# Three of four sums of weight blocks added by the loads themselves, and delayed sums of gated values, in a transformer trunk of two layers

## The chip, the cores and the metric

The kernel runs on one core of one Trainium2 chip. The metric is the device time of one execution in microseconds. TensorE (PE), VectorE (DVE), ScalarE (ACT), GpSimd (POOL) and SyncE (SP) each work through a program of their own; in this kernel SP and POOL also issue the DMAs spoken of here, each on a queue of its own.

## The reference

Two layers are applied to x, 1024 rows of 1024 values in float32; then a last normalisation.

```python
for l in range(DEPTH):
    x = x + hybrid_mixer(rms_norm(x, mix_norm[l]), ...)
    x = x + memory_cross_attention(rms_norm(x, mem_x_norm[l]), mem, ...)
    x = x + conv_gated_ffn(rms_norm(x, ffn_norm[l]), ffn_w_up[l], ffn_conv_w[l], ffn_conv_b[l], ffn_w_down[l])
return rms_norm(x, final_norm)

def conv_gated_ffn(h, w_up, conv_w, conv_b, w_down):
    a = h @ w_up
    ap = jnp.pad(a, ((0, 0), (1, 1), (0, 0)))
    a = ap[:, :-2] * conv_w[0] + ap[:, 1:-1] * conv_w[1] + ap[:, 2:] * conv_w[2] + conv_b
    gate, val = a[..., :D_FF], a[..., D_FF:]
    return (jax.nn.silu(gate) * val) @ w_down
```

The mixer has six latent attention heads, six grouped query heads and a gated part; D_FF is 2816.

## The kernel before

Each float32 operand is split into a high and a low part, and each product of two operands is three matmuls (high by high, high by low, low by high). The working memory in SBUF is 46 slots of 128 x 1024 floats, handed out by the class `Slots` in the order in which they came free. A framework schedules the program: it orders each engine's instructions itself, from the order of the code and the times that it reckons with, so code that moves in one place can reorder an engine elsewhere.

**A layer.** One combined projection comes first, then the attention: 24 items (12 heads by two groups of 512 queries) swept by `attention` (L332). Beside each item it runs side work from a table `fill`, and, in the third of an item's four steps, what the table `extra` holds for that item (L360). In an item POOL scales the rows of the probabilities (L305), which PE then transposes (L140). POOL also does parts of the rotary step for the coming heads (L621 to L627) and of the output's scaling (L682). Then come the output projection, the memory attention, and the FFN, in which the change lies.

**The FFN's up phase.** The two products of the FFN are each computed with seven block products in place of eight. w_up comes as four blocks b0 to b3, each 22 columns of 128 wide; a column is a tile of 128 x 512 floats, 256 KB. The seven products m = 1 to 7 of column j need on the side of the weights:

| m | weights | m | weights |
|---|---|---|---|
| 1 | b0 | 5 | b2 + b3 |
| 2 | b1 | 7 | b0 + b2 |
| 4 | b3 | 6 | b0 + b2 + b3 |
| | | 3 | b0 + b1 + b2 + b3 |

On the side of the activations `NormS.make(m)` forms sums and differences and splits them. The list `order` puts the products (j, m): columns 0 and 1 side by side at first, then a column after the other in the order 1, (4 of the column before), 6, 5, 2, 7, 3. One step of the loop at L1299 does this: `fetch()` (L1082) loads a column of 256 KB into half a slot; `make_w()` (L1091) makes the operand of the product four places on, its high part on ACT (L1096) and its low part on DVE (L1097); `product(j, m)` issues 12 matmuls (L1143 to L1145); `post(j, m)` takes the product out of its bank (ACT L1159 for m = 1, L1165 for m = 2; DVE for the others, L1171 for m = 7); and the convolution, the gating and `keep` of finished columns are worked off a list `todo`. Five columns are fetched before the FFN begins (FETCH - AHEAD), and two at a time in the first four steps.

**The sums of blocks.** `Blocks` (L781) computes all four sums ahead, in DRAM, in parts of two to four columns (up to 1 MB; UP_PARTS, DOWN_PARTS). For each sum and part SP copies one block (L796) and POOL adds another by a DMA that accumulates onto the copy (L801); 6 is made by adding 5, and 3 by adding 6. For w_up each layer runs 24 copies and 24 adds during its attention, from `extra`. For w_down (11 columns, parts of 3, 4 and 4) it runs 12 copies in the attention, and the 12 adds come later, one at every product m = 5 of the up phase from column 2 on (`add_later`). The copies carry a dependence on the last L305 in the code so that the scheduler doesn't issue them sooner. POOL does little else in the FFN: the reciprocal roots of the norm (L132) and the issuing of DMAs.

**The gated values.** `keep(j)` (L1210) stores the gated column's halves to DRAM by SP (L1213), seven stores for each pair of columns, and forms four sums of those pieces by accumulating DMAs on POOL (L1216), issued right behind the stores in the code.

**The down phase.** `down` goes through (m, i), 11 columns i for each m in the order 1, 5, 6, 3, 7, 2, 4. `fetch_d` (L1223) loads a piece of the gated values and a column of w_down or of its sums, eight places ahead; `make_d` (L1230) splits both on ACT and DVE, four places ahead; `d_mm` (L1252) does the 12 matmuls (L1256).

Of the kernel before, what the change touches and what calls it, by code (L numbers as in the profile page):

```python
# [8 lines left out]
F32 = mybir.dt.float32  # L9
F32R = mybir.dt.float32r  # L10
AF = mybir.ActivationFunctionType
ALU = mybir.AluOpType
AX = mybir.AxisListType

P = 128
# [54 lines left out]
def trunk(ctx: ExitStack, tc: tile.TileContext, a: dict, out: bass.AP):  # L70
# [313 lines left out]
    def layer(l, nt, w_m, last):  # L384
# [396 lines left out]
        class Blocks:  # L781

            def __init__(self, w, parts, name):
                self.w, self.parts, self.at = w, parts, [sum(parts[:i]) for i in range(len(parts))]
                self.sum = {
                    (m, i): dpool.tile([P, n * CH + 16], F32, tag=f"{name}{l}_{m}_{i}", name=f"{name}{l}_{m}_{i}")[:, : n * CH]
                    for m in (5, 6, 7, 3) for i, n in enumerate(parts)
                }  # L790

            def piece(self, b, i):
                return self.w[b][:, self.at[i] * CH : (self.at[i] + self.parts[i]) * CH]

            def copy(self, m, i):
                c = nc.sync.dma_start(self.sum[m, i], self.piece({5: 2, 6: 0, 7: 0, 3: 1}[m], i))  # L796
                tc.add_manual_dep(ins_of(c), ins_of(Item.last).name, mybir.DependencyInfo(mybir.DependencyClass.Sync, mybir.DependencyReason.DATA), reason="not sooner")

            def add(self, m, i):
                src = self.sum[{6: 5, 3: 6}[m], i] if m in (6, 3) else self.piece({5: 3, 7: 2}[m], i)  # L800
                tc.keep_in_program_order(nc.gpsimd.dma_start(self.sum[m, i], src, accum_op=ALU.add))  # L801

            def block(self, m, j):
                if m in (1, 2, 4):
                    return self.w[{1: 0, 2: 1, 4: 3}[m]][:, j * CH : (j + 1) * CH]
                i = max(i for i in range(len(self.parts)) if self.at[i] <= j)
                return self.sum[m, i][:, (j - self.at[i]) * CH : (j - self.at[i] + 1) * CH]

            def steps(self):
                n = len(self.parts)  # L810
                return [(self, m, i + o) for i in range(0, n, 2) for m, o in ((5, 0), (5, 1), (7, 0), (6, 0), (6, 1), (7, 1), (3, 0), (3, 1)) if i + o < n]

# [56 lines left out]

        extra, steps = {}, w_u.steps()  # L870
        for n, (w, m, i) in enumerate(steps):
            g = n * 18 // len(steps)
            extra.setdefault(g, []).append(lambda w=w, m=m, i=i: w.copy(m, i))
            extra.setdefault(g + 3, []).append(lambda w=w, m=m, i=i: w.add(m, i))
        later = deque(sorted(w_d.steps(), key=lambda s: (5, 7, 6, 3).index(s[1])))
        for n, (w, m, i) in enumerate(later):
            extra.setdefault(n * 20 // len(later), []).append(lambda w=w, m=m, i=i: w.copy(m, i))

        def add_later():
            if later:  # L880
                w, m, i = later.popleft()
                w.add(m, i)

# [198 lines left out]
        def fetch():  # L1082

            if (jm := next(fetched, None)) is not None:
                if not half:
                    z = sl.get(F32)
                    half.extend([(quarter(z, 0), None), (quarter(z, 1), z)])
                raws[jm] = half.pop(0)
                nc.sync.dma_start(raws[jm][0], w_u.block(jm[1], jm[0]))

# [9 lines left out]

        for _ in range(FETCH - AHEAD):
            fetch()
# [107 lines left out]
        def keep(j):  # L1210
            z, i = st.pop(j)["cg"], j // 2
            for q, h in ((("21", 1), ("u4", 1), ("22", 0), ("u2", 0)) if j % 2 else (("11", 1), ("u1", 0), ("u3", 0))):
                nc.sync.dma_start(gq[q, i], quarter(z, h))  # L1213
            sl.put(z)
            for q, p in ((("u3", "22"), ("u2", "u1"), ("u4", "u2")) if j % 2 else (("u1", "11"),)):
                nc.gpsimd.dma_start(gq[q, i], gq[p, i], accum_op=ALU.add)  # L1216

# [5 lines left out]
        def fetch_d():  # L1223
            if (mi := next(d_fetch, None)) is not None:
                m, i = mi
                z = d_raw[mi] = sl.get(F32)
                nc.sync.dma_start(quarter(z, 0), gq[{1: "11", 2: "21", 3: "22", 4: "u4", 5: "u1", 6: "u2", 7: "u3"}[m], i])
                nc.sync.dma_start(quarter(z, 1), w_d.block(m, i))

# [34 lines left out]
        def down(after0, after1, tail):  # L1264

            for m, i in d_order:
# [20 lines left out]
                for _ in range(2):  # L1287
                    if todo:
                        todo.popleft()()
                if i == NP - 1:  # L1290
                    for t in range(TPC):
                        d_add(m, t)
                        if m == 7:
                            after0(t)
                    if m == 2 and tail:
                        tail(None)

        early = deque()
        for i, (j, m) in enumerate(order):  # L1299
            for _ in range(1 + (i < AHEAD)):  # L1300
                fetch()
            for _ in range(1 + (i < AHEAD)):
                make_w()
            product(j, m)
            post(j, m)
            if (j, m) == (0, 2):
                ns.turn(1, range(0, 4))
                ns.turn(1, range(4, 8))
                ns.make(5)
            if m == 5 and j > 1:  # L1310
                add_later()
# [190 lines left out]
```

## Time and profile before

| | |
|---|---|
| time, median of three runs | 2774.91 us (2772.91 to 2776.51) |
| profiled execution, its time | 2770.64 us |
| its span | 2768.8 us |
| granted clock | 0.998 |
| busy: PE, DVE, ACT, POOL | 98%, 70%, 53%, 26% |
| DMA packets' time on SP's queue, on POOL's | 34.6%, 18.2% of the engines' span |
| HBM read, written | 371.75 MB, 206.05 MB |

The profile is one execution, taken by the hardware profiler; its own time is compared with its span, not with the median. The windows view gives the busy time of each engine in a stretch of the span; the waits name what ended an engine's idle time; the chain is the work that ended last, followed back; the timeline lists an engine's instructions. Attention of the first layer runs from about 130 to 480 us of the span, of the second from 1505 to 1855; the up phase of the first layer's FFN from about 745 to 1175, its down phase up to 1385. L12 is line 12 of the kernel.

### The profile page before, as it was taken

To read this page: it belongs to the slowest core of one execution; us is meant where nothing else is said; L and a number is where in the kernel's file an instruction comes from. 1 tells how busy PE (TensorE), PEld (TensorE's weight loads), DVE (VectorE), ACT (ScalarE), POOL (GpSimd) and SP (SyncE) were. 2 spreads that over 40 slices of the span, in tenths; PEclk is the share of its full clock that TensorE was granted. 3 is DMA by queue.
4 is the path that set the end of the run, shared out by engine and by line. 5 is a ranking of instruction groups with operands and counts; after the bars stand their busy time and mean duration, and the time that the engine had idled before them with its cause. 6 is when DMAs were issued, how large, how long until landed. Compare 5 with 4: busy or idle time off the path is not lost.

```text
span 2768.8 us, 37951 instructions
## 1 busy us (share of the span) xinstructions
PE 2724.2 (98%) x13648; PEld 2284.4 (83%) x13648; DVE 1941.6 (70%) x2905; ACT 1470.8 (53%) x2838; POOL 706.3 (26%) x744
## 2 busy tenths in 40 slices
PE   9999999999999999999999999999999999999998
PEld 7997888888878888888889877888888888888887
DVE  5489879556697777774445888894666877778754
ACT  4378978224554444553333888881345544446432
POOL 3245676320001110000123456662200011100000
PEclk9999999999999999999999999999999999999999
DMA  4027994221159875785210289831221698767752
GB/s 147 27 80 199 263 233 97 73 69 62 46 150 237 223 213 166 225 272 183 88 59 19 83 232 265 220 83 61 70 68 46 173 239 225 204 169 244 247 187 102
DMA packets 160748, 418.80 MB, mean 151 GB/s; under 512 B 17840, under 2 KB 18480, under 8 KB 146224
## 3 DMA queue, kind: packets, MB, share of 16 engines
q1 hardware_dynamic: 137376, 323.84, 34.6%
q0 software_dynamic: 23040, 92.28, 18.2%
q8 instruction: 107, 1.75, 0.2%
q14 instruction: 81, 0.66, 0.1%
q10 hardware_dynamic: 144, 0.26, 0.0%
HBM read 371.75 MB, written 206.05 MB: 209 GB/s over the span
## 4 chain that ended last, share of the span: by engine, by line
PE 85%; DVE 5%; ACT 3%; DMA 3%; POOL 2%; issue 1%; SPq 0%; POOLq 0%; DVEq 0%; ACTq 0%
PE bank L1256 8%; PE bank L116 7%; PE bank L118 7%; PE bank L117 7%; PE bank L140 7%; PE pair L1256 6%; PE bank L1144 5%; PE bank L1145 5%; PE bank L1143 5%; PE pair L1143 4%; PE pair L1144 4%; PE pair L1145 4%; PE bank L318 3%; PE bank L319 3%; PE pair L116 2%; PE pair L118 2%
## 5 line engine op out<-in xcount | busy, mean ns | idle before, releaser
L124 DVE TENSOR_TENSOR s<-bank,s 128x512 fp32r<-128x512 f32 (+3 forms) x552 | 331.5, 630 | 116.4 <-ACT s L123 112.7
L116 PE MATMUL bank<-s,s 128*128 128x512 f32 (+4 forms) x1124 | 404.2, 360 | 4.6 <-DVE s L124 3.4
L118 PE MATMUL bank<-s,s 128*128 128x512 f32 (+4 forms) x1124 | 399.5, 356 | 1.1 <-DVE s L111 0.9
L117 PE MATMUL bank<-s,s 128*128 128x512 f32 (+4 forms) x1124 | 398.4, 355 | 0.3 <-DVE s L111 0.3
L123 ACT ACTIVATE s<-bank 128x512 fp32r<-128x512 f32 (+3 forms) x552 | 286.0, 556 | 205.7 <-PE bank L140 142.5
L140 PE MATMUL bank<-ident,s 128*128 128x128 f32 (+1 forms) x2320 | 324.0, 274 | 17.5 <-POOL s L305 6.3
L140 PEld LDWEIGHTS bank<-ident,s 128*128 128x128 f32 (+1 forms) x2320 | 270.1, 140 | 77.7 <-DVE s L124 9.6
L1096 ACT ACTIVATE s<-s 128x512 fp32r<-128x512 f32 x308 | 187.5, 627 | 181.5 <-PE bank L1145 46.1
L1144 PE MATMUL bank<-s,s 128*128 128x512 f32 x704 | 274.5, 390 | 0.9 <-DVE s L209 0.9
L1145 PE MATMUL bank<-s,s 128*128 128x512 f32 x704 | 273.9, 389 | 0.0
L1143 PE MATMUL bank<-s,s 128*128 128x512 f32 x704 | 273.7, 389 | 0.0
L305 POOL TENSOR_SCALAR s<-s,stat 128x1024 f32<-128x1024 f32 x192 | 222.8, 1160 | 184.4 <-DVE stat L304 136.5
L295 DVE TENSOR_REDUCE stat<-pair 128x1 f32<-128x1024 f32 x192 | 233.5, 1216 | 39.6 <-PE pair L118 19.0
L132 POOL TENSOR_TENSOR stat<-stat,mhalf 128x1 f32<-128x1 f32 (+3 forms) x94 | 84.3, 897 | 634.3 <-DVE stat L131 634.1
L1256 PE MATMUL bank<-s,s 128*128 128x512 f32 (+1 forms) x1068 | 242.7, 387 | 1.6 <-DVE stat L131 1.6
L116 PEld LDWEIGHTS bank<-s,s 128*128 128x128 f32 x1124 | 211.7, 189 | 33.6 <-DVE s L124 3.7
L1241 DVE TENSOR_TENSOR s<-s,s 128x512 fp32r<-128x512 f32 x264 | 170.6, 685 | 93.1 <-ACT s L1240 93.1
L1256 PEld LDWEIGHTS bank<-s,s 128*128 128x128 f32 x1068 | 198.7, 188 | 42.3 <-DVE x L1347 1.8
L118 PEld LDWEIGHTS bank<-s,s 128*128 128x128 f32 x1124 | 211.7, 188 | 26.3 <-DVE s L111 1.3
L117 PEld LDWEIGHTS bank<-s,s 128*128 128x128 f32 x1124 | 212.1, 189 | 24.1 <-DVE s L111 0.6
L1240 ACT ACTIVATE s<-s 128x512 fp32r<-128x512 f32 x264 | 153.9, 623 | 140.9 <-DMA s<-g_u 47.3
L1097 DVE TENSOR_TENSOR s<-s,s 128x512 fp32r<-128x512 f32 x308 | 201.7, 686 | 36.2 <-ACT s L1096 33.9
(182 smaller groups left out, 5521.0 us busy)
## 6 DMA issues: line engine op xcount, KB each, us to landing
s<-u SPq DMA_DIRECT2D x176, 256.0 KB, 4.3
u<-in_w_up SPq DMA_DIRECT2D x40, 1024.0 KB, 13.3
s<-in_w_up SPq DMA_DIRECT2D x132, 256.0 KB, 4.4
g_u<-s SPq DMA_DIRECT2D x88, 256.0 KB, 3.0
s<-g_u SPq DMA_DIRECT2D x88, 256.0 KB, 3.3
s<-d SPq DMA_DIRECT2D x88, 256.0 KB, 3.6
u<-in_w_up POOLq DMA_DIRECT2D x20, 1024.0 KB, 18.4
u<-u POOLq DMA_DIRECT2D x20, 1024.0 KB, 13.3
```

The lines of the kernel that those rows point to most:

```text
L116: nc.tensor.matmul(o, l[0], r[0], start=first, stop=False)
L117: nc.tensor.matmul(o, l[0], r[1], start=False, stop=False)
L118: nc.tensor.matmul(o, l[1], r[0], start=False, stop=last)
L123: nc.scalar.activation(hi, src, AF.Copy)
L124: nc.vector.tensor_tensor(lo, src, f(hi), ALU.subtract)
L140: nc.tensor.transpose(b[:m, j * P : (j + 1) * P], s, ident)
L295: nc.vector.reduce_max(self.nm[:, 0:1], s, axis=AX.X, negate=True)
L305: Item.last = nc.gpsimd.tensor_scalar(p, p, r[:, 0:1], 0.0, ALU.mult, ALU.add)
L1143: nc.tensor.matmul(o, lh, rh, start=k == 0 and m in (1, 5, 6), stop=False, skip_group_check=True)
L1144: nc.tensor.matmul(o, lh, rl, start=False, stop=False, skip_group_check=True)
L1145: nc.tensor.matmul(o, ll, rh, start=False, stop=k == 3, skip_group_check=True)
L1256: nc.tensor.matmul(o, lh[p], rh[q], start=m in (1, 5, 2) and i == 0 and k == 0, stop=i == NP - 1 and k == 2, skip_group_check=True)
```

## The change

Only the sum for m = 6 is still made ahead in DRAM: per part one copy of b0, then b2 and b3 added. For w_up that is 6 copies and 12 adds a layer, spread over the attention's items by another rule; for w_down 3 copies in the attention and 6 adds, one at the product m = 5 of every even column from 2 on. The three other sums are made when a column is loaded (`load`): SP loads one block's column into the slot (b2, b0, or the ready sum), and POOL accumulates the second (b3, b2, or b1) onto it from DRAM by a DMA. In all 66 such accumulations of 256 KB in the up phase of a layer and 33 in its down phase. `keep` puts its sums into a list `due`; `add_due` issues them three, six and nine steps later, both in the up and the down phase. And four columns, not five, are fetched before the FFN begins.

```diff
-            def copy(self, m, i):
-                c = nc.sync.dma_start(self.sum[m, i], self.piece({5: 2, 6: 0, 7: 0, 3: 1}[m], i))
+            def copy(self, i):
+                c = nc.sync.dma_start(self.sum[i], self.piece(0, i))
...
-            def add(self, m, i):
-                src = self.sum[{6: 5, 3: 6}[m], i] if m in (6, 3) else self.piece({5: 3, 7: 2}[m], i)
-                tc.keep_in_program_order(nc.gpsimd.dma_start(self.sum[m, i], src, accum_op=ALU.add))
...
+            def add(self, i, b):
+                tc.keep_in_program_order(nc.gpsimd.dma_start(self.sum[i], self.piece(b, i), accum_op=ALU.add))
...
+            def load(self, z, m, j):
+
+                first, *second = {1: (0,), 2: (1,), 4: (3,), 6: (4,), 5: (2, 3), 7: (0, 2), 3: (4, 1)}[m]
+                nc.sync.dma_start(z, self.col(first, j))
+                if second:
+                    nc.gpsimd.dma_start(z, self.col(second[0], j), accum_op=ALU.add)
...
-        extra, steps = {}, w_u.steps()
-        for n, (w, m, i) in enumerate(steps):
-            g = n * 18 // len(steps)
-            extra.setdefault(g, []).append(lambda w=w, m=m, i=i: w.copy(m, i))
-            extra.setdefault(g + 3, []).append(lambda w=w, m=m, i=i: w.add(m, i))
-        later = deque(sorted(w_d.steps(), key=lambda s: (5, 7, 6, 3).index(s[1])))
-        for n, (w, m, i) in enumerate(later):
-            extra.setdefault(n * 20 // len(later), []).append(lambda w=w, m=m, i=i: w.copy(m, i))
+        extra, later = {}, deque((w_d, i, b) for b in (2, 3) for i in range(len(DOWN_PARTS)))
+        for i in range(len(UP_PARTS)):
+            extra.setdefault(2 * i, []).append(lambda i=i: w_u.copy(i))
+            for n in range(2):
+                extra.setdefault(2 * i + 4 + 3 * n, []).append(lambda i=i, n=n: w_u.add(i, 2 + n))
+        for i in range(len(DOWN_PARTS)):
+            extra.setdefault(13 + 2 * i, []).append(lambda i=i: w_d.copy(i))
...
-                nc.sync.dma_start(raws[jm][0], w_u.block(jm[1], jm[0]))
+                w_u.load(raws[jm][0], jm[1], jm[0])
...
-        for _ in range(FETCH - AHEAD):
+        for _ in range(AHEAD):
             fetch()
...
-            for q, p in ((("u3", "22"), ("u2", "u1"), ("u4", "u2")) if j % 2 else (("u1", "11"),)):
-                nc.gpsimd.dma_start(gq[q, i], gq[p, i], accum_op=ALU.add)
+            for n, (q, p) in enumerate((("u3", "22"), ("u2", "u1"), ("u4", "u2")) if j % 2 else (("u1", "11"),)):
+                due.append((step[0] + 3 + 3 * n, lambda q=q, p=p, i=i: nc.gpsimd.dma_start(gq[q, i], gq[p, i], accum_op=ALU.add)))
+
+        due, step = deque(), [0]
+
+        def add_due(all=False):
+
+            while due and (all or due[0][0] <= step[0]):
+                due.popleft()[1]()
...
-                nc.sync.dma_start(quarter(z, 1), w_d.block(m, i))
+                w_d.load(quarter(z, 1), m, i)
...
+                step[0] += 1
+                add_due(not todo)
...
+            step[0] = i
             for _ in range(1 + (i < AHEAD)):
                 fetch()
+            add_due()
...
-            if m == 5 and j > 1:
+            if m == 5 and j > 1 and j % 2 == 0:
                 add_later()
```

In the kernel after, L801 of `Blocks.add` is L798, the loads of a column are L809 (SP) and L811 (POOL's accumulation), L1096 is L1095, L1159 and L1165 are L1158 and L1164, L1216 is L1215.

Three places show how the change moves instructions. The first is POOL in the first layer's attention, at one of the piles of work ahead of a scaling that PE waits for; u is a part of w_up's sums, s a slot, L682 and L621 to L627 the steps named above. Before:

```order
L801 DMA u_3_2_1629<-u_6_2_1617 128x2048
L305 TENSOR_SCALAR s_340_3877<-s_340_3877,stat 128x1024
L682 TENSOR_TENSOR s_318_3676<-s_318_3676,s_344_3928 128x1024
L621 TENSOR_TENSOR s_348_3966<-s_141_1705,s_73_703 128x128
L622 TENSOR_TENSOR s_348_3966<-s_141_1705,s_73_703 128x128
L623 TENSOR_TENSOR s_348_3966<-s_141_1705,s_73_703 128x128
L625 TENSOR_TENSOR s_348_3966<-s_141_1705,s_73_703 128x128
L626 TENSOR_TENSOR s_141_1705<-s_348_3966 128x8x16
L305 TENSOR_SCALAR s_343_3922<-s_343_3922,stat 128x1024
L627 TENSOR_TENSOR s_141_1705<-s_348_3966 128x8x16
L305 TENSOR_SCALAR s_347_3960<-s_347_3960,stat 128x1024
```

The same place on POOL after the change:

```order
L798 DMA u_3_1612<-in_w_up 128x2048
L305 TENSOR_SCALAR s_340_3824<-s_340_3824,stat 128x1024
L682 TENSOR_TENSOR s_318_3626<-s_318_3626,s_344_3874 128x1024
L621 TENSOR_TENSOR s_348_3912<-s_141_1678,s_73_703 128x128
L622 TENSOR_TENSOR s_348_3912<-s_141_1678,s_73_703 128x128
L623 TENSOR_TENSOR s_348_3912<-s_141_1678,s_73_703 128x128
L625 TENSOR_TENSOR s_348_3912<-s_141_1678,s_73_703 128x128
L626 TENSOR_TENSOR s_141_1678<-s_348_3912 128x8x16
L627 TENSOR_TENSOR s_141_1678<-s_348_3912 128x8x16
L305 TENSOR_SCALAR s_343_3868<-s_343_3868,stat 128x1024
L305 TENSOR_SCALAR s_347_3906<-s_347_3906,stat 128x1024
```

The DMA at the head stays with another source; L627 has moved ahead of the scaling behind which it stood.

The second place is POOL at the start of the first layer's FFN; L110 makes rows of the norm, L132 is the reciprocal root of a row block's mean square, g_u and d are sums of gated values and of w_down. Before:

```order
L110 TENSOR_SCALAR s_660_7281<-s_659_7280 128x1024
L110 TENSOR_SCALAR s_663_7287<-s_662_7286 128x1024
L132 TENSOR_TENSOR stat<-stat,mhalf 128x1 x8
L1216 DMA g_u_0_7786<-g_11_0_7753 128x512
L801 DMA d_5_0_1633<-in_w_down 128x1536
L1216 DMA g_u_0_7808<-g_22_0_7775 128x512
```

The same place on POOL after the change:

```order
L110 TENSOR_SCALAR s_660_7215<-s_659_7214 128x1024
L110 TENSOR_SCALAR s_663_7221<-s_662_7220 128x1024
L811 DMA s_698_7762<-in_w_up 128x512 x2
L132 TENSOR_TENSOR stat<-stat,mhalf 128x1 x7
L811 DMA s_706_7812<-in_w_up 128x512 x2
L811 DMA s_714_7901<-in_w_up 128x512 x2
L132 TENSOR_TENSOR stat<-stat,mhalf 128x1
L811 DMA s_732_8031<-in_w_up 128x512
L811 DMA s_740_8086<-in_w_up 128x512 x2
L811 DMA s_752_8180<-in_w_up 128x512
L798 DMA d_0_1615<-in_w_down 128x1536
```

Six accumulations, for the products (0, 5), (1, 5), (0, 3), (1, 3), (0, 7) and (1, 7), now stand ahead of the eighth L132, four of them directly.

The third place is ACT at the same time: it makes operands (L1096, after it L1095) between the copies of product banks (L1159 and L1165, after it L1158 and L1164). Before:

```order
L1159 ACTIVATE s_702_7852<-bank 128x512
L1096 ACTIVATE s_719_7989<-s_703_7855 128x512
L1096 ACTIVATE s_721_8008<-s_703_7855 128x512
L1096 ACTIVATE s_726_8046<-s_707_7879 128x512
L1159 ACTIVATE s_706_7876<-bank 128x512
L1096 ACTIVATE s_735_8112<-s_715_7966 128x512
L1165 ACTIVATE s_710_7899<-bank 128x512
L185 ACTIVATE s_681_7601<-bank,cols_86 128x512
```

ACT at that place after the change:

```order
L1158 ACTIVATE s_701_7786<-bank 128x512
L1095 ACTIVATE s_719_7928<-s_706_7812 128x512
L1095 ACTIVATE s_720_7946<-s_706_7812 128x512
L1095 ACTIVATE s_726_7985<-s_714_7901 128x512
L1158 ACTIVATE s_705_7810<-bank 128x512
L1164 ACTIVATE s_709_7835<-bank 128x512
L185 ACTIVATE s_680_7533<-bank,cols_86 128x512
```

The operand of slot s_714, the one for (0, 7), is made at the same place as before, but its block is now the sum of two transfers; the L185 that scale the turned rows stand two copies behind it. The operand between the two copies has moved further back.

More of the change, by code (lines that the diff above doesn't have):

```diff
@@ L786, in __init__ @@
                 self.w, self.parts, self.at = w, parts, [sum(parts[:i]) for i in range(len(parts))]
[L787 to L790, printed above, removed]
+                self.sum = [dpool.tile([P, n * CH + 16], F32, tag=f"{name}{l}_{i}", name=f"{name}{l}_{i}")[:, : n * CH] for i, n in enumerate(parts)]
@@ L803, in block @@
-            def block(self, m, j):
-                if m in (1, 2, 4):
-                    return self.w[{1: 0, 2: 1, 4: 3}[m]][:, j * CH : (j + 1) * CH]
-                i = max(i for i in range(len(self.parts)) if self.at[i] <= j)
[L807 to L811, printed above, removed]
+            def add(self, i, b):
+                tc.keep_in_program_order(nc.gpsimd.dma_start(self.sum[i], self.piece(b, i), accum_op=ALU.add))
@@ new lines, in col @@
+            def col(self, b, j):
+                if b < 4:
+                    return self.w[b][:, j * CH : (j + 1) * CH]
+                i = max(i for i in range(len(self.parts)) if self.at[i] <= j)
+                return self.sum[i][:, (j - self.at[i]) * CH : (j - self.at[i] + 1) * CH]
+            def load(self, z, m, j):
[3 more added lines that the diff above has]
+                    nc.gpsimd.dma_start(z, self.col(second[0], j), accum_op=ALU.add)
@@ L867, in layer @@
         fill[23] += [lambda: y_split(1, 1, 2)]
-        extra, steps = {}, w_u.steps()
-        for n, (w, m, i) in enumerate(steps):
-            g = n * 18 // len(steps)
-            extra.setdefault(g, []).append(lambda w=w, m=m, i=i: w.copy(m, i))
-            extra.setdefault(g + 3, []).append(lambda w=w, m=m, i=i: w.add(m, i))
-        later = deque(sorted(w_d.steps(), key=lambda s: (5, 7, 6, 3).index(s[1])))
-        for n, (w, m, i) in enumerate(later):
-            extra.setdefault(n * 20 // len(later), []).append(lambda w=w, m=m, i=i: w.copy(m, i))
+        extra, later = {}, deque((w_d, i, b) for b in (2, 3) for i in range(len(DOWN_PARTS)))
[5 more added lines that the diff above has]
+            extra.setdefault(13 + 2 * i, []).append(lambda i=i: w_d.copy(i))
         def add_later():
             if later:
-                w, m, i = later.popleft()
-                w.add(m, i)
+                w, i, b = later.popleft()
+                w.add(i, b)
         w_o = {}
```

## The prediction

> **What bounds the kernel now.** I read the page's head first, then the windows view by stage, then the waits, then the chain and the timeline where PE stands still.
>
> ```profile
> span 2768.8 us, 37951 instructions
> PE 2724.2 (98%) x13648; PEld 2284.4 (83%) x13648; DVE 1941.6 (70%) x2905; ACT 1470.8 (53%) x2838; POOL 706.3 (26%) x744
> ```
>
> PE is busy for 2724.2 of 2768.8 us, so 44.6 us is all that any change in the transfers can win, and the change removes no matmul. The windows view shows where that idle time lies (columns: stretch, its length, busy us and instructions of PE, PEld, DVE, ACT, POOL, granted clock, DMA share, GB/s):
>
> ```profile
> 130.00:480.00 350.00, 341.21 (x1960) 287.50 (x1959) 298.54 (x484) 283.89 (x620) 217.62 (x210) 1.00 0.65 170
> 756.00:860.00 104.00, 100.60 (x445) 81.53 (x445) 88.63 (x125) 57.70 (x85) 10.01 (x12) 1.00 0.65 174
> 860.00:1010.00 150.00, 150.00 (x660) 123.36 (x659) 108.66 (x141) 67.99 (x94) 19.90 (x24) 1.00 0.88 223
> 1010.00:1170.00 160.00, 160.00 (x704) 131.38 (x704) 117.03 (x155) 76.02 (x110) 13.13 (x16) 1.00 0.66 195
> 1505.00:1855.00 350.00, 341.65 (x1953) 287.56 (x1952) 298.48 (x483) 283.97 (x619) 215.74 (x210) 1.00 0.65 170
> ```
>
> The attention of each layer (first and last row) leaves PE idle for 8.8 and 8.4 us; the first 104 us of the FFN's up phase for 3.4; the 310 us behind them for nothing, though the DMA share reaches 0.88 there. So the attention can gain a little, and the up phase, where the change puts its new transfers, can only lose.
>
> **The change part by part.**
>
> *Attention: half of POOL's accumulating DMAs go.* A layer issues 12 in place of 24 here. The windows view of L801 alone, POOL's waits, and the place of PE's largest wait, by the chain and the timeline:
>
> ```profile
> 130.00:480.00 350.00, 20.11 (x24) 1.00 0.65 170
> PE bank L140 <- POOL s L305: 6.3, 4, 2.5
> 347.76 2.37 POOL s L682
> ...
> 352.21 1.12 POOL s L305
> 353.30 0.45 POOL L627 TENSOR_TENSOR s<-s 128x128 f32<-128x128 f32 x1
> 353.38 0.76 PE L140 MATMUL bank<-ident,s 128*128 128x128 f32 x5 [2.50 <-POOL s L305]
> 1727.36 1.14 PE L140 MATMUL bank<-ident,s 128*128 128x128 f32 x5 [2.50 <-POOL s L305]
> ```
>
> 24 issues hold POOL for 20.11 us, 0.84 each, so 12 fewer free 10.1 us of its 217.6. But PE waited for POOL only 6.3 us in the whole program, and 5.0 of that are the two waits of 2.50 us, one in each layer. What runs on POOL ahead of them is L682 (2.37 us), the small steps L621 to L626 and the scaling L305; no DMA stands in that chain, so taking DMAs out doesn't shorten it. By the order of instructions the step L627 (0.45 us) now stands ahead of the scaling that PE waits for, where it stood behind: +0.45 us a layer, +0.9 in all. For the other waits I take −1 us of the remaining 1.3 us on POOL, a little less than all of it. Bounds of this term: −6.3 (all waits on POOL go) and +3 (one more step of 0.84 to 1.12 us in each pile). Taken: −0.1.
>
> *Start of the FFN: the accumulations stand ahead of the last rows' norm on POOL.* The order puts six issues of L811 ahead of the eighth L132 (the reciprocal root of the last 128 rows), and the two for products (0,7) and (1,7) ahead of nothing but ACT. The timeline of before:
>
> ```profile
> 744.05 0.84 SPq L1089 DMA_DIRECT2D s<-u  x2
> 744.94 1.30 SPq L1089 DMA_DIRECT2D s<-in_w_up  x2
> 748.82 0.93 POOL L132 TENSOR_TENSOR stat<-stat,mhalf 128x1 f32<-128x1 f32 x1 [7.12 <-DVE stat L131]
> 749.23 1.68 ACT L1096 ACTIVATE s<-s 128x512 fp32r<-128x512 f32 x3
> 754.04 0.60 ACT L1165 ACTIVATE s<-bank 128x512 f32<-128x512 f32 x1 [0.44 <-PE bank L1145]
> 754.54 3.00 ACT L185 ACTIVATE s<-bank,cols 128x512 f32<-128x512 f32 x5
> s<-in_w_up SPq DMA_DIRECT2D x132, 256.0 KB, 4.4
> g_u<-g POOLq DMA_DIRECT2D x44, 256.0 KB, 5.5
> ```
>
> POOL had been idle 7.12 us ahead of that L132, so the first accumulations find room; the last two wait for loads issued at about 744.5 us, which land 4.4 us later (748.9). L132 behind them is late by about one issue, 0.84 us or a little over. The sum for (0,7) is there 5.5 us after its issue, at 754.4. By the new order ACT makes that operand's high part, then copies two product banks, then starts the eight L185 that split the turned rows. Three instructions of about 0.5 us from 754.4 put L185 at 755.9 in place of 754.54: +1.4 us a layer, +2.8 in all, since PE has no other work there (3.4 us idle in the window from 756). Bounds 0 (the loads are issued earlier than I think) and +3 a layer (one product's time more).
>
> *Up phase: 66 small accumulations a layer come in, six of w_down's twelve large sums go.* The DMA view of 860 to 1010 us, and the loads' margins:
>
> ```profile
> q0 software_dynamic: 3510, 12.25, 45.2%
> q1 hardware_dynamic: 11548, 21.03, 42.2%
> d<-d POOLq DMA_DIRECT2D x4, 1024.0 KB, 10.8
> d<-in_w_down POOLq DMA_DIRECT2D x2, 1024.0 KB, 10.1
> d<-d POOLq DMA_DIRECT2D x2, 768.0 KB, 9.3
> 1132.89 0.42 SPq L1089 DMA_DIRECT2D s<-in_w_up  x1
> 1156.62 0.62 ACT L1096 ACTIVATE s<-s 128x512 fp32r<-128x512 f32 x1
> 1172.49 0.39 PE L1143 MATMUL pair<-s,s 128*128 128x512 f32 x1
> 1175.37 29.92 PE bank L1256 x132
> ```
>
> Queue 0 (POOL's) held the engines for 45.2% of 150 us = 67.8 us for 12.25 MB, 5.53 us a MB, so a block of 256 KB (0.262 MB) costs 1.45 us. Queue 1 (SP's) took 63.3 us for 21.03 MB: 0.79 us a block. An accumulation onto a block in SBUF isn't in the trace. Its bounds: 0.79 (it costs a plain load), and 67.8 / 24 = 2.8 us, if all of queue 0's time went by the piece (POOL's 24 instructions in that window are its issues). I take 1.45: most of those pieces are accumulations of just this size on just this queue. Eight sums for w_down, 6 × 1.049 + 2 × 0.786 = 7.86 MB or 43.5 us, 29.0% of the window, become four or so: −14.5 points. Three accumulations every seven products come in: a product is 12 matmuls, 29.92 / 11 = 2.72 us, so 150 us hold 150 / 19.04 × 3 = 23.6 of them, 34.3 us, +22.8 points. Share: 87.4 − 14.5 + 22.8 = 95.7%. It fits, and reaches 100% at a price of (100 − 72.9)% × 150 / 23.6 = 1.72 us. With 0.79 the share would be 85%.
>
> What covers the longer way of a block: the last load of the phase goes out at 1132.89, is made into an operand at 1156.62 and multiplied from 1172.49. Of the 23.7 us up to ACT, the shorter lookahead (four fetches ahead in place of five) takes 2.7; load, issue and accumulation take 4.4 + 0.8 + 5.5 = 10.7. So 10.3 us are left before ACT would wait at all, and 15.9 more before PE would. Cost at the share of 0.96: 0.
>
> *Down phase: 33 accumulations a layer onto w_down's blocks.* The windows view and ACT's waits:
>
> ```profile
> 1170.00:1385.00 215.00, 214.28 (x951) 176.79 (x949) 128.04 (x200) 92.73 (x158) 12.47 (x15) 1.00 0.56 182
> ACT s L1240 <- DMA s<-g_u: 47.3, 29, 3.5
> ```
>
> The share is lower (0.56), blocks are fetched as far ahead as before, and ACT already waits for loads here (47.3 us) while PE stands only 0.7 us of 215: the operands are made well ahead. Cost 0, or up to the 0.7 us again in each layer.
>
> *The late loads of 853 us.* PE's only other stops in the up phase:
>
> ```profile
> 853.49 0.50 PE L1143 MATMUL pair<-s,s 128*128 128x512 f32 x1 [1.52 <-DVE s L1171]
> 2228.45 0.50 PE L1143 MATMUL pair<-s,s 128*128 128x512 f32 x1 [0.48 <-DVE s L1171]
> s<-in_w_up SPq DMA_DIRECT2D x4, 256.0 KB, 9.6
> d<-in_w_down POOLq DMA_DIRECT2D x2, 1024.0 KB, 12.9
> ```
>
> The last two rows are the DMA view of 820 to 845 us: loads took 9.6 us beside two sums of 1 MB, and 8 us later PE waited. With half as many such sums I take half of 1.52 + 0.48 back: −1.0 (bounds −2.0 and 0).
>
> *Delayed sums of the gated values.* POOL stands in line for each store to land before it can issue the sum:
>
> ```profile
> POOL g_u L1216 <- DMA g<-s: 599.1, 40, 53.6
> ```
>
> Nothing else needed POOL then. With the accumulations of L811 on the same queue such a wait would hold them up, and issuing the sums three products (8.2 us) after the stores removes it; cover is POOL's idleness, 87% of the window from 860. Cost 0. Their last readers come a phase later.
>
> **The sum.** −0.1 + 2.8 + 0 − 1.0 = +1.7 us on the profiled execution's 2770.64 (span 2768.8). The median of the runs, 2774.91, stands 4.27 us over that execution, so the forecast is 2770.64 + 1.7 + 4.27 = 2776.6 us. About 0.2%, 5.5 us, is what a measurement of this kernel can tell from no change; this is inside it.
>
> **The rivals.**
>
> *Slower: blocks come late behind the large sums.* POOL's queue is served in order: an accumulation issued behind a 1 MB sum (10.8 us) lands that much later, beyond the 10.3 us left before ACT waits; ACT, which also empties the product banks, then holds PE as at 853. The new order still has six such sums a layer among the accumulations. Each costing what the first of those stops did: 12 × 1.52 = 18.2 us, so 2793. Decides from an accumulation price of about 1.7 us, where the queue no longer catches up. For it: the share is already 0.88, the two stops exist. Against: 15.9 us more until PE. Chance 0.25.
>
> *Faster: POOL's relief counts in full.* If the scheduler's shifted order lets the piles at 347 and 1721 us start earlier, the 6.3 us on POOL go, and with fewer large sums both stops as well: −8.3, so 2766.6. For it: 10.1 us less of issues on an engine that is 62% busy in the attention. Against: POOL had stood idle ahead of that pile, and the pile grows by L627. Chance 0.13.
>
> *Accumulations cost by the piece.* At 2.8 us each the window's share would be 87.4 − 4 × 2.8 / 1.5 + 23.6 × 2.8 / 1.5 = 124%, and 0.66 + 0.44 = 110% from 1010 to the last load at 1133. Backlog 36 + 12 = 48 us, less the 26 that cover it: 22 us a layer, 44 in all, 2820. Against it: a sum of 1 MB took 10.8 us to land and one of 256 KB 5.5, so bytes count. Chance 0.04. The Trainium skill states such a rule, page "DMA: Bandwidth & Descriptors", section "Anatomy of one DMA — SWDGE (gpsimd) path": a GpSimd DMA takes about 2.0 us and its bytes over 436 GB/s, an estimate of 2.6 us for 256 KB. By that, taken as engine time, the up phase would fall behind as in this rival, by less; the same section puts most of the 2 us down to the receipt of the last write, which leaves the engines free, and queue 0's 24 pieces in 67.8 us leave at most 2.8 us each.
>
> **How the numbers follow.** Forecast 0.58, late blocks 0.25, relief in full 0.13, by the piece 0.04. The range takes in the forecast's term bounds upwards (0 to +3 a layer at the FFN's start, +3 in the attention) and the late blocks, 2793; downwards it stops at 2768.0, short of the relief in full. It leaves out 0.17. Faster by over 0.2%: 0.13; within: 0.58; slower: 0.25 + 0.04 = 0.29.
>
> **What would show it.** Right: PE's waits on L305 stay at 2.5 us or grow to about 2.95; L185 at the FFN's start begins 1 to 2 us later; DMA share 0.93 to 0.97 from 860 to 1010 with PE without a gap; loads' users wait less than 20 us in sum. Wrong: PE idle in windows that had none, put down to ACT or DVE behind DMA; PE's idle time in the attention down by several us a layer.

## The result, and the profile after

The changed kernel takes 2859.22 us (median of four runs, 2854.43 to 2862.58), the kernel before 2773.92 (four runs): ratio 1.0307, 95% interval 1.0295 to 1.0319. That is 85 us slower, and outside the range of the prediction. The head of the page of the kernel after:

```profile
span 2857.7 us, 38270 instructions
PE 2742.2 (96%) x13648; PEld 2295.8 (80%) x13648; DVE 1937.8 (68%) x2905; ACT 1465.5 (51%) x2838; POOL 849.8 (30%) x906
```

The span is 88.9 us longer; PE's idle time has grown from 44.6 to 115.5 us, and PE is busy 18 us longer with the same 13648 matmuls. The first matmul of the up phase and of the down phase in each layer cut the span into five stretches (us, worked out from the trace; the same cuts serve the experiments):

```
kernel   to up phase, layer 0 | up phase 0 | down 0 to up phase 1 | up phase 1 | rest
before                 745.68 |     429.53 |               945.94 |     429.22 | 218.46
after                  748.91 |     469.71 |               948.87 |     471.83 | 218.35
```

The two up phases hold 82.8 us of the 88.9. The attention and what lies between it and the FFN's first product are in the 6.2 us of the first and third column, and the down phase, with 66 accumulations, costs nothing. The windows view of after, in the stretches shown of before, except that the last row is the first layer's down phase as it now lies:

```profile
130.00:480.00 350.00, 339.79 (x1949) 288.26 (x1948) 297.02 (x481) 282.80 (x617) 206.31 (x197) 1.00 0.27 63
756.00:860.00 104.00, 90.15 (x389) 73.01 (x388) 80.99 (x115) 53.61 (x80) 18.06 (x21) 0.93 0.69 164
860.00:1010.00 150.00, 136.13 (x584) 109.90 (x584) 95.83 (x125) 60.41 (x85) 33.97 (x39) 0.99 0.90 213
1010.00:1170.00 160.00, 153.33 (x671) 125.06 (x670) 109.97 (x144) 68.56 (x96) 35.65 (x41) 1.00 0.87 210
1218.70:1433.00 214.30, 213.47 (x953) 175.79 (x951) 125.77 (x198) 90.02 (x156) 40.02 (x48) 1.00 0.73 216
```

In the attention the DMA share has fallen from 0.65 to 0.27, and PE has gained nothing from it. From 860 to 1010 us PE, before without a gap, stands 13.9 us. The down phase runs at a share of 0.73, and PE stands 0.8 us of 214.3; in the kernel before it stood 0.9 us of the same phase (1175.3 to 1389.6 us), at a share of 0.54. The waits view names who is waited for (total, times, longest):

```profile
PE pair L1142 <- DVE s L1170: 32.5, 13, 9.5
PE pair L1142 <- DVE s L1168: 26.9, 12, 4.5
PE bank L140 <- POOL s L305: 13.3, 8, 2.9
ACT s L1095 <- DMA s<-in_w_up: 210.3, 60, 11.1
```

PE doesn't wait for an operand, but for a product bank that DVE has not emptied: L1168 and L1170 are `post` for m = 7 and m = 4, L1169 and L1171 in the kernel before (the description above gives L1171 to m = 7; it is the line for m = 4). The fourth row tells why: ACT, making operands (L1095), waits 210 us for blocks; in the kernel before, ACT's waits for blocks at this line were 16.2 us in nine cases. One stop, followed back by the chain of waits (start, us, what):

```profile
884.68 0.64 ACT s L1095
...
887.09 12.49 DMA s<-in_w_up
899.67 0.64 ACT s L1095
900.37 0.57 issue
900.94 0.68 DVE s L1162
901.62 0.61 DVE s L1206
902.26 6.88 DMA s<-in_w_up
...
910.91 0.70 DVE s L1096
911.63 0.64 ACT s L1095
912.33 0.57 issue
912.90 0.69 DVE s L1168
913.64 0.50 PE pair L1142
```

An accumulation that takes 12.49 us holds ACT, ACT holds DVE (L1096 needs the high part), a second accumulation holds both again, and only then comes L1168, for which PE has stood since 909. The operands themselves are not late: the one of this stop's product, (6, 4), was made 28 us before its use. POOL's queue in the same stretch, by the timeline:

```profile
885.50 1.14 POOL L798 DMA_DIRECT2D d<-in_w_down  x1
887.09 0.91 POOL L811 DMA_DIRECT2D s<-in_w_up  x1 [0.46 <-DVE s L1096]
900.45 0.88 POOL L811 DMA_DIRECT2D s<-in_w_up  x1 [12.45 <-DMA s<-in_w_up]
902.26 0.86 POOL L811 DMA_DIRECT2D s<-in_w_up  x1 [0.94 <-DVE s L1206]
```

The first accumulation goes out right behind a sum of 1 MB, and the next one waits 12.45 us on POOL for its own load, which is as slow. Both theories that I started from are in these rows: the order on the queue, and the engines' time.

### The profile page after: what moved, and what is told of

It reads as the page before. It is cut to its first block, busy times and chain, and to the rows that moved or that the text cites. A ratio compares the mean times of both kernels' runs of the same rounds, so it can differ in the third digit from the quotient of the medians.

```text
span 2857.7 us, 38270 instructions
## 1 busy us (share of the span) xinstructions
PE 2742.2 (96%) x13648; PEld 2295.8 (80%) x13648; DVE 1937.8 (68%) x2905; ACT 1465.5 (51%) x2838; POOL 849.8 (30%) x906
## 4 chain that ended last, share of the span: by engine, by line
PE 68%; DVE 10%; DMA 9%; ACT 6%; issue 3%; POOL 3%; SPq 0%; ACTq 0%; POOLq 0%; DVEq 0%
PE bank L1262 8%; PE bank L116 7%; PE bank L118 7%; PE bank L117 7%; PE bank L140 6%; PE pair L1262 6%; DMA s<-in_w_up 6%; PE pair L1142 2%; PE bank L1143 2%; PE bank L1144 2%; PE pair L116 2%; PE bank L318 2%; PE pair L118 2%; PE bank L319 2%; PE bank L1142 2%
## 5 line engine op out<-in xcount | busy, mean ns | idle before, releaser
L1095 ACT ACTIVATE s<-s 128x512 fp32r<-128x512 f32 x308 | 187.9, 626 | 369.3 <-DMA s<-in_w_up 210.3
L140 PE MATMUL bank<-ident,s 128*128 128x128 f32 (+1 forms) x2320 | 322.2, 275 | 29.7 <-POOL s L305 13.3
L1096 DVE TENSOR_TENSOR s<-s,s 128x512 fp32r<-128x512 f32 x308 | 208.1, 688 | 167.8 <-ACT s L1095 166.0
L305 POOL TENSOR_SCALAR s<-s,stat 128x1024 f32<-128x1024 f32 x192 | 219.0, 1141 | 197.2 <-DVE stat L304 151.5
L1142 PE MATMUL pair<-s,s 128*128 128x512 f32 x528 | 213.9, 405 | 62.2 <-DVE s L1170 32.5
L116 PEld LDWEIGHTS bank<-s,s 128*128 128x128 f32 x1124 | 212.2, 189 | 31.9 <-DVE s L124 3.0
L1247 DVE TENSOR_TENSOR s<-s,s 128x512 fp32r<-128x512 f32 x264 | 170.3, 687 | 96.7 <-ACT s L1246 96.5
L118 PEld LDWEIGHTS bank<-s,s 128*128 128x128 f32 x1124 | 212.0, 189 | 26.8 <-DVE s L111 1.7
L811 POOL DMA_DIRECT2D s<-in_w_up x132 | 121.0, 970 | 376.6 <-DMA s<-in_w_up 108.8
L1262 PEld LDWEIGHTS bank<-s,s 128*128 128x128 f32 x1068 | 198.7, 188 | 42.3 <-DVE x L1357 1.8
## 6 DMA issues: line engine op xcount, KB each, us to landing
u<-in_w_up POOLq DMA_DIRECT2D x20, 1024.0 KB, 10.3
```

Source lines behind the costliest of these rows:

```text
L116: nc.tensor.matmul(o, l[0], r[0], start=first, stop=False)
L118: nc.tensor.matmul(o, l[1], r[0], start=False, stop=last)
L140: nc.tensor.transpose(b[:m, j * P : (j + 1) * P], s, ident)
L305: Item.last = nc.gpsimd.tensor_scalar(p, p, r[:, 0:1], 0.0, ALU.mult, ALU.add)
L1142: nc.tensor.matmul(o, lh, rh, start=k == 0 and m in (1, 5, 6), stop=False, skip_group_check=True)
L1262: nc.tensor.matmul(o, lh[p], rh[q], start=m in (1, 5, 2) and i == 0 and k == 0, stop=i == NP - 1 and k == 2, skip_group_check=True)
```

## The experiments

All are compared with the kernel before on the same chip. **Theory A**: accumulations stand in line on POOL behind large sums, stores and their own loads, and a longer lead would cover it. **Theory B**: the DMA engines are full, whatever the order. The first four runs were made to tell them apart.

**w_down's large sums moved into the attention.**

```diff
-            extra.setdefault(13 + 2 * i, []).append(lambda i=i: w_d.copy(i))
+            extra.setdefault(3 + 4 * i, []).append(lambda i=i: w_d.copy(i))
+            for n in range(2):
+                extra.setdefault(3 + 4 * i + 4 + 4 * n, []).append(lambda i=i, n=n: w_d.add(i, 2 + n))
+        later.clear()
```

> The changed kernel with w_down's six large sums of a layer moved from the up phase into the attention, where the DMA share has fallen to 0.27. Theory A (order: an accumulation stands in line on POOL behind large sums and behind stores that have not landed; ACT and DVE, in line themselves, then bring the product banks back late): the large sums are a good part of that line, so most of the 85 us goes: 2785 to 2810. Theory B (throughput: the DMA engines are full in the up phase): the share there falls by about a tenth and the time to 2800 to 2820. If neither the large sums nor the share matters: 2850 to 2860.

2840.42 us, ratio 1.0242 (1.0227 to 1.0257): 19 us better than the change, outside all three ranges. The up phases take 459.6 and 457.0 us, still 58 us over before, and ahead of them 8 us more are lost than in the changed kernel. The large sums are a part, and not the greater one.

**The second transfer overwrites in place of adding.**

```diff
-                    nc.gpsimd.dma_start(z, self.col(second[0], j), accum_op=ALU.add)
+                    nc.gpsimd.dma_start(z, self.col(second[0], j))
```

> The changed kernel, but the second transfer of a block overwrites the first in place of adding to it (so the sums of blocks are left out); same queue, same waits, same bytes read, no read of the destination. Theory A (order on the queues): within 10 us of the changed kernel, 2850 to 2865. Theory B (throughput): the second transfer costs the engines about 0.8 us in place of 1.65, 13 points of share from 860 to 1010 us, and the time falls to 2790 to 2810.

2803.66 us, 1.0108 (1.0091 to 1.0125): 56 us better, as theory B had it. The windows view and the DMA view of 860 to 1010 us of this kernel:

```profile
860.00:1010.00 150.00, 146.55 (x643) 119.84 (x642) 104.77 (x138) 65.86 (x91) 29.56 (x42) 1.00 0.84 233
s<-in_w_up POOLq DMA_DIRECT2D x23, 256.0 KB, 4.0
```

The share is 0.84, but the second transfer also lands sooner: 4.0 us after its issue, where the accumulation takes 6.0 there. So the run does not tell engine time from landing time.

**w_up's sums in DRAM as before; accumulation onto loaded blocks for w_down alone.**

```diff
-        w_u = Blocks([a["w_up"][l, b] for b in range(4)], UP_PARTS, "u")
+        w_u = Sums([a["w_up"][l, b] for b in range(4)], UP_PARTS, "u")
...
-                w_u.load(raws[jm][0], jm[1], jm[0])
+                nc.sync.dma_start(raws[jm][0], w_u.block(jm[1], jm[0]))
```

(`Sums` is the class `Blocks` of the kernel before, with its steps in `extra`.)

> The changed kernel, but w_up's four sums are made ahead in DRAM in the attention as in the kernel before; accumulation onto loaded blocks is left for w_down alone. Both theories: the up phase is as before, so 2768 to 2782. Over 2790 would mean that the down phase's accumulations or the delayed sums of gated values cost something that the windows don't show.

2781.12 us, 1.0027 (1.0016 to 1.0038). This is inside the range expected. All but 7 us of the loss comes with w_up's accumulations. What is left lies for the most part in the up phases too (434.3 and 434.8 us in the profiled execution, 4.8 and 5.6 over before), where this kernel still has the shorter lookahead and the delayed sums; the stretch with the first down phase is 0.2 us longer.

**Four more fetches ahead.**

```diff
-        for _ in range(AHEAD):
+        for _ in range(2 * AHEAD):
             fetch()
```

> The changed kernel with eight first fetches in place of four, so that each block is fetched four products (10.9 us) earlier. Theory A (the longer way of a block, load and then accumulation, exceeds the time that ACT's order leaves for it): the waits go for the most part, 2785 to 2815. Theory B (throughput): the same bytes have to pass in the same time, 2845 to 2860.

2852.75 us, 1.0289 (1.0274 to 1.0304): theory A's number failed, and theory B's was met. But the rows of L1095 in this kernel (what ended ACT's idle time before it; us, times) show that the blocks were no longer late:

```profile
  DMA g_u<-s: 111.4, 32
  PE pair L1144: 85.7, 52
```

ACT now waits for the slot into which it is to write the operand: for stores of gated values that still read it, and for products that do. The earlier fetches hold two slots more, so each slot comes round sooner. One wait had taken another's place, so this run had not tested the lead. **Theory C** came out of it: a block's two transfers end after the moment at which ACT, in its fixed order, turns to the block; what is needed is time between load and making, without more slots.

**Operands made two products ahead, in place of four, and four more fetches.**

```diff
-        for _ in range(AHEAD):
+        for _ in range(2 * AHEAD):
             fetch()
...
-            for _ in range(1 + (i < AHEAD)):
+            for _ in range(1 + (i < 2)):
                 make_w()
```

> The changed kernel with operands made two products ahead in place of four and eight first fetches in place of four: the two slots that the makes give up are those that the fetches take, so a block has six products (16 us) more between its load and its making, and no more slots are in use. Theory C (a block's two transfers end after the moment that ACT's order has for it; ACT and DVE then hold everything behind it): ACT's waits for blocks go and the time falls to 2785 to 2815. Theory B (the engines' throughput bounds the up phase): 2840 or more, since the bytes are the same.

2783.27 us, 1.0036 (1.0023 to 1.0049), just under the range of theory C: 76 of the 85 us are gone, with all the accumulations and all the large sums in their places. The windows view and the DMA view from 860 to 1010 us, and the row of L1095's waits for blocks:

```profile
860.00:1010.00 150.00, 150.00 (x661) 123.48 (x661) 108.45 (x141) 65.75 (x93) 38.10 (x44) 1.00 0.98 243
q0 software_dynamic: 6266, 14.30, 54.9%
q1 hardware_dynamic: 12048, 21.95, 43.0%
s<-in_w_up POOLq DMA_DIRECT2D x24, 256.0 KB, 7.6
  DMA s<-in_w_up: 1.3, 1
```

The DMA engines are fuller than in any other run (0.98), an accumulation lands later than in the changed kernel (7.6 us), and PE does not stand at all. Theory B falls with this: the share bounded nothing. ACT waits 1.3 us for blocks in place of 210.3. Counting loads on SP, accumulations on POOL and makes on ACT in their order gives the median times of a block with two transfers (the 31st to the 140th block of each layer; us; single pairs can be wrong by a place, since four of the 96 for the changed kernel come out below zero):

```
kernel                          load issue to   accumulation   load issue
                                both landed     to making      to making
before (one transfer)                -               -            13.8
after                               13.7             1.1          14.8
two ahead only                      12.2             4.2          17.7
four more fetches only              10.3            19.7          30.2
two ahead, four more fetches        14.7            18.0          32.8
```

In the changed kernel ACT starts 1.1 us after the accumulation lands: it stood there waiting.

**The later making alone.**

```diff
-            for _ in range(1 + (i < AHEAD)):
+            for _ in range(1 + (i < 2)):
                 make_w()
```

> The changed kernel with operands made two products ahead in place of four, first fetches left at four: half of what the run before last changed, with two slots less in use. Theory C: blocks have about two products (5.4 us) more before ACT turns to them, of the 6 to 12 us by which they were late, so between half and all of the loss goes: 2785 to 2825. If it was the earlier fetches alone that helped: 2850 or more.

2823.85 us, 1.0185 (1.0171 to 1.0199): 35 us back, at the upper end of what theory C gave. With a median of 4.2 us to spare, the slower blocks still came late (ACT waits 59.5 us for them).

**Both edits on the kernel before, as a control.**

```diff
-        for _ in range(FETCH - AHEAD):
+        for _ in range(2 * AHEAD):
             fetch()
...
-            for _ in range(1 + (i < AHEAD)):
+            for _ in range(1 + (i < 2)):
                 make_w()
```

> The kernel before with the same two edits (operands two products ahead, eight first fetches). Theory C: the kernel before has two stops of 1.5 and 0.5 us from late loads, so it gains these at most: 2768 to 2775. If operands made only two products ahead cost PE waits by themselves: 2778 to 2790, and the version of the changed kernel with both edits is to be read with that in mind.

2779.3 us, 1.0022 (1.0013 to 1.0031): 6 us slower, not faster, so the second expectation holds. The stop at 853 us is gone, but each up phase is 2.2 to 2.5 us longer, with new stops of 1.07 and 1.11 us at 776 and 790 us that the version of the changed kernel with both edits has as well. So of the 9 us by which the changed kernel with both edits is over before, a part is the price of the edits.

**The first block alone, without the second transfer.**

```diff
-                if second:
-                    nc.gpsimd.dma_start(z, self.col(second[0], j), accum_op=ALU.add)
```

> The changed kernel without the second transfer: products 5, 7 and 3 take the first block alone (the accumulations onto loaded blocks are left out). What is left over the kernel before is the attention's new order, the FFN's start, the shorter lookahead and the delayed sums. Theory C: 2776 to 2784. If the delayed sums or the lookahead cost much by themselves: over 2795.

2783.24 us, 1.0039 (1.0023 to 1.0054), as theory C had it. The accumulations' whole price in the changed kernel is 2859 − 2783 = 76 us, and the version with both leads, which has them all, takes the same time as this one without any. The 9 us that are left here, with neither accumulations nor new leads, belong to the rest of the change.

**What stands in line on POOL.** Three more runs took up theory A's parts. The sums of gated values right behind their stores again:

```diff
-                due.append((step[0] + 3 + 3 * n, lambda q=q, p=p, i=i: nc.gpsimd.dma_start(gq[q, i], gq[p, i], accum_op=ALU.add)))
+                nc.gpsimd.dma_start(gq[q, i], gq[p, i], accum_op=ALU.add)
```

> The changed kernel with the sums of gated values issued right behind their stores, as in the kernel before. If waits for stores on POOL hold the accumulations behind them: slower than the changed kernel by 10 us or more (2870 to 2900). If that line doesn't matter: 2855 to 2863.

2871.0 us, 1.0357 (1.0326 to 1.0387): 12 us worse than the change, so that line does hold the accumulations up. Put off further instead (`step[0] + 9 + 3 * n`):

> The changed kernel with the sums of gated values put off by nine, twelve and fifteen steps in place of three, six and nine. POOL still waited 247 us for their stores in the changed kernel, with accumulations behind. If that holds blocks up: 2825 to 2850. If not: 2855 to 2863.

2859.3 us, 1.0294 (1.0271 to 1.0316): no difference. And w_down's sum in parts of one column:

```diff
-UP_PARTS, DOWN_PARTS = (2, 4, 4, 4, 4, 4), (3, 4, 4)
+UP_PARTS, DOWN_PARTS = (2, 4, 4, 4, 4, 4), (1,) * 11
...
-            extra.setdefault(13 + 2 * i, []).append(lambda i=i: w_d.copy(i))
+            extra.setdefault(12 + i, []).append(lambda i=i: w_d.copy(i))
...
-            if m == 5 and j > 1 and j % 2 == 0:
+            if m == 5 and j > 1:
                 add_later()
+                if j in (3, 5):
+                    add_later()
```

> The changed kernel with w_down's sum made in eleven parts of 256 KB in place of three of up to 1 MB: the same bytes, 20 of the 22 additions still in the up phase, but none longer than an accumulation. If the length of the transfer in front is what made blocks late: as good as moving them away, 2835 to 2845. If their bytes are: 2855 to 2863.

2857.6 us, 1.0299 (1.0284 to 1.0314): the length of the transfer in front doesn't matter. That its bytes do is what the expectation leaves over; moving them away gave 19 us. The delay of the gated sums that the change brings is worth 12 us of what it would otherwise lose; more delay brings nothing.

**Four ahead for columns 0 and 1, two from there on.**

```diff
-            for _ in range(1 + (i < AHEAD)):
+            for _ in range(1 + (i < AHEAD) - (i in (14, 16))):
                 make_w()
```

(with the four more fetches)

> The changed kernel with eight first fetches, operands made four products ahead for columns 0 and 1 as before and two ahead from there on. The version that makes two ahead throughout was left 9 us over the kernel before; its up phases were 5.5 us each longer, with stops of 1.1 us at 776 and 789 us. If these belong to the short lead at the start: 2774 to 2780. If the first columns then run out of slots or blocks as in the run with earlier fetches alone, whose stop at 831 us was 8.7 us: 2790 to 2805.

2785.49 us, 1.0048 (1.0034 to 1.0063): between the two expectations, and in neither. One of the two stops of 1.1 us went, and one of 2.98 us came at 821 us. No version that was run beats the kernel before.

## Why the prediction was wrong

**The step that failed** is the cover of a block's longer way: "Of the 23.7 us up to ACT ... 10.3 us are left before ACT would wait at all, and 15.9 more before PE would." It failed in both halves. The 23.7 us came from the last load of the phase, whose issue followed the one ahead of it at once. Mid-phase SP's loads wait for slots that PE is still reading (L1089 behind L1145's products: 102.6 us in 22 waits from 860 to 1170 us), and the time from issue to making is shorter. Loads on SP, makes on ACT and products on PE matched by their count, these are the rows of product (10, 7) in the timeline of the kernel before (the load is the first of the two):

```profile
923.82 0.80 SPq L1089 DMA_DIRECT2D s<-u  x2
934.87 0.63 ACT L1096 ACTIVATE s<-s 128x512 fp32r<-128x512 f32 x1 [0.22 <-PE bank L1145]
956.43 0.39 PE L1143 MATMUL pair<-s,s 128*128 128x512 f32 x1
```

This block has 11.1 us from issue to making, and the median of mid-phase blocks is 13.8. That is about what the program gives: five places at 2.72 us a product are 13.6 us, and four are 10.9. The sum with that: 13.8 − 2.7 for the shorter lookahead − 10.7 = 0.4 us, so nothing was left. The transfers were longer too, 13.7 us for 10.7; in the run without the second transfer, which is hardly held up, the same blocks have 12.6 us from issue to making, less than two transfers take. And the "15.9 more" were never cover: from the moment ACT waits for a block, the copies, convolutions and operands behind it in its order wait as well, DVE with them, and PE stops at the next bank that DVE should have emptied, with operands in store for 20 us. The rival "blocks come late" named that very path; I gave it 0.25 and 18.2 us, by a stop of 1.52 us at each large sum. There was no need of a large sum (without them the up phases still lost 58 us), a stop came in nearly every pair of columns, and with what the FFN's start takes of it the up phases lost 82.8 us. The −1.0 us for the late loads at 853 us failed with the same step: at 831 us PE now stands 9.54 us.

**The throughput** was right and misled. A share of 95.7% was forecast at full pace; the version with both leads shows 0.98 at full pace. The price of 1.45 us a block, an average over all of queue 0, is 1.51 in that run (54.9% of 150 us for 14.30 MB, 5.76 us a MB) and 1.65 in the changed kernel (53.1% for 12.66 MB). Below the 1.72 us from which the queue was to fall behind, the loss came all the same: the point of decision was the lead, not the share.

**By the piece** falls: 44 issues (POOL's count in the window of that run) at 2.8 us would be 123 us, where the queue held the engines for 82.4. By the rule of the Trainium skill, page "DMA: Bandwidth & Descriptors", section "Anatomy of one DMA — SWDGE (gpsimd) path", taken as engine time, the fixed 2.0 us alone would come to 88 us, an estimate; the trace stands with the section's own remark that the fixed part is mostly the wait for a receipt.

**Attention**: −0.1 us was forecast. PE's waits on L305 rose from 6.3 to 13.3 us. The pile is as forecast, by the chain of the kernel after:

```profile
352.09 0.45 POOL s L627
352.54 1.11 POOL s L305
353.65 0.04 issue
353.69 0.77 PE bank L140 x5
```

L627 stands ahead of the scaling and the stop is 2.92 us for 2.50. The relief elsewhere did not come; other stops on L305 (1.87 and 1.03 us in each layer) are new. The total, 3 us a layer up to the FFN's first product, cannot be put down to the change alone: the control, whose attention code is that of the kernel before, shows +3.3 and +1.1 us in the same columns.

**The FFN's start**: +1.4 us a layer was forecast, by L185 behind the block of (0, 7). The timeline of the kernel after:

```profile
756.47 0.63 ACT L1095 ACTIVATE s<-s 128x512 fp32r<-128x512 f32 x1 [3.89 <-DMA s<-in_w_up]
759.04 0.77 PE L140 MATMUL bank<-ident,s 128*128 128x128 f32 x5 [1.48 <-DVE s L147]
760.60 1.97 ACT L185 ACTIVATE s<-bank,cols 128x512 f32<-128x512 f32 x3
760.77 1.51 PE L140 MATMUL bank<-ident,s 128*128 128x128 f32 x6 [0.95 <-ACT s L1164]
```

Counted from the first product (748.91, before 745.68), L185 is 2.8 us later, and PE stands 1.48 + 0.95 us where it did not (1.03 + 1.65 in the second layer): mechanism right, size twice the forecast. The price of the **down phase**, 0, was right, with its accumulations at a share of 0.73. The **delayed sums** were to end POOL's wait for the stores; it fell from 599.1 to 246.8 us, and the delay avoids 12 us. That it costs nothing is not shown: the run with w_up's sums in DRAM and the one without the second transfer both hold it, together with the shorter lookahead, and are 7 and 9 us over before.

**Still open**: what makes the last 9 us of the version with both leads (the control, with the same leads, is 6 us over by itself, mostly ahead of and in the up phases; the changed kernel without the second transfer is 9 us over with neither lead), and whether a lead in the first columns that needs no more slots would bring it level.

## What to carry to other kernels

A transfer that becomes two in a row needs a longer lead at the engine that consumes it, and the lead must be measured on blocks in mid-phase, from load issue to first use, not on the last one. Here 20 us of finished operands did not cover ACT's wait for a block, because everything else in ACT's order waited with it. The DMA engines were 98% busy at no cost where the lead was long; before taking bytes away, move the consumer later and the load earlier, and count the slots that both hold.

## What the runs showed of the hardware

In the two up phases PE's idle time grows from 6 to 70 us, 64 of the 82.8; in the other 19 the profile has PE busy. About 10 of these are matmuls at half pace behind a stop, by the timeline of the kernel after (what the rest is was not worked out):

```profile
830.73 0.79 PE L1142 MATMUL pair<-s,s 128*128 128x512 f32 x1 [9.54 <-DVE s L1170]
831.32 0.63 PE L1143 MATMUL pair<-s,s 128*128 128x512 f32 x1
831.75 0.63 PE L1144 MATMUL pair<-s,s 128*128 128x512 f32 x1
...
836.46 0.39 PE L1143 MATMUL bank<-s,s 128*128 128x512 f32 x1
836.69 0.39 PE L1144 MATMUL bank<-s,s 128*128 128x512 f32 x1
```

Matmuls start 0.43 us apart for some 5 us and 0.23 apart after. Each of the six stops of 3.03 us or more in the up phases is followed by such a stretch of 7 to 11 matmuls, 52 in all, at 0.20 us each 10.4 us; a stop of 2.51 us and the shorter ones past the FFN's start are not. It is the granted clock, which these rows of the windows view of after give as 0.50 (the third figure from the end):

```profile
760.84:764.25 3.41, 3.41 (x16) 3.23 (x17) 3.15 (x5) 3.07 (x5) 0.92 (x1) 0.50 0.89 280
825.69:835.93 10.24, 5.20 (x12) 4.12 (x13) 7.42 (x9) 5.38 (x7) 3.48 (x4) 0.50 0.90 165
914.44:917.85 3.41, 3.41 (x9) 2.65 (x8) 2.70 (x4) 2.02 (x3) 0.00 (x0) 0.50 0.94 178
```

The trace has the clock at half in seven stretches of the up phases: five of 3.41 us and, at the two longest stops, two of 10.24 us, which began before PE went on. The first row stands at the FFN's start, at the two stops of 1.48 and 0.95 us. The Trainium skill, page "TensorE: Matmul & The Clock Gate", section "Part 1: The HAM clock gate", has the clock halved after an idle window of about 3.4 us and restored after as long a busy one. The lengths of 3.41 us and three times that agree with it; but a single stop of 3.03 us, and the two short ones, brought a stretch too, and there the measurement decides.

An accumulation of 256 KB from DRAM onto a block in SBUF landed 5.9 us after its issue in the changed kernel (median, mid-phase), where a plain transfer on the same queue took 4.1 in the run that overwrites (DMA shares 0.90 and 0.84 from 860 to 1010 us).
